# Where q leaves PSUM, where the weight parts are made, and where single steps stand, in a hybrid attention layer

## The chip, the cores and the metric

The kernel runs on one core of one Trainium2 chip. The metric is the device time of one execution in microseconds (us), lower is better. A NeuronCore has five engines with instruction streams of their own: TensorE (PE; its weight loads are listed as PEld), VectorE (DVE), ScalarE (ACT), GpSimd (POOL) and SyncE (SP). Here SyncE and GpSimd issue most of the DMA transfers. Each engine takes its instructions in the order in which the program has them, and waits on semaphores for the others.

## The reference

One layer of a decoder trunk, for 1024 tokens of width 2048, in float32. Cut to what is computed:

```python
hn = rmsnorm(h, norm_mix_g)
sb_q, sb_k, sb_v, sb_g, df_q, df_k, df_v, df_g = split(hn @ w_in)          # eight times 1024 columns
# 8 stick-breaking heads of 128: z = q k / sqrt(128), masked to s < t;
#   w = sigmoid(z_ts) * prod over s<j<t of (1 - sigmoid(z_tj));  out = w @ v
# 8 differential heads, two q/k pairs of 64 each, rotary on the first 16 of each:
#   a = softmax(q1 k1 / 8) - lam * softmax(q2 k2 / 8), causal;  out = a @ v, then rmsnorm over the head
mixed = concatenate([sb_out * silu(sb_g), df_out * silu(df_g)])
h = h + mixed @ w_out
gate = sigmoid(rmsnorm(h, norm_ple_g) @ w_ple_gate)
h = h + gate * (p @ w_ple_proj)
return rmsnorm(h, norm_final_g)
```

## The kernel before, in words

Every large product is done on pairs of numbers. An operand x is cast to a reduced format by ScalarE (the high part, names ending in h or hi), VectorE subtracts that from x (the low part, l or lo), and TensorE adds three products: high by high, high by low, low by high. So each operand costs a 128x512 cast, a 128x512 subtraction and two tiles.

The kernel has four stages.

1. **The seven-product stage for v and g** (class `Seven`, object `gv`, up to about 620 us). It computes the v and gate columns for both halves of the tokens with seven block products instead of eight (A11, A12, S1 to S4, A22), in two phases over the inner dimension and over 16 output units. One product is one *slot* of 12 matmuls. At the end of each slot `step` makes the high and low part of one more weight block (`whigh`, `wlow`), runs what is due, and takes up to two entries of a list of loads and splits. A ring of ten tiles holds the weight parts.
2. **The heads of the first half of the tokens** (`half == 1` in the code; its k and v are kept for the second), about 620 to 1085 us, and then **of the second half** (`half == 0`), to about 1660 us. Heads go in the order `ORDER`: differential head 8, stick-breaking head 0, 9, 1, ..., 15, 7. `unit` computes a head's q and k columns into two PSUM banks (`acc[0]` for q, `acc[1]` for k; the tag has two buffers, so the next head's q product needs the bank that this head's q leaves) in 32 groups of three matmuls. After each group `side.tick()` advances a counter and calls those steps of a sorted list whose tick has come. All other work (casts, scores, softmax, transposes, loads) hangs on that list: `side.add` puts steps at given ticks, `side.later(dt, fn)` puts one dt ticks on. So the attention of a head is done within the product groups of the next two to three heads, and what is called earlier stands earlier in each engine's stream. Equal ticks keep the order in which they were added.
3. **The output projection**, a second `Seven` (`op`). Its first 64 groups (A11 and A12 of eight output units) still carry the last head's attention; their results `hc` go to DRAM.
4. The gate product and the end.

What the change touches, with the lines of the profile:

- `wprep` and `split` load a head's weights (`wraw`, 512 KB), cast them (L162, ScalarE) and, in the first half of the tokens, subtract for the low part (L158, VectorE, 128x1024) and store it in `wlo_d`. The second half loads that stored low part (L164).
- `taken(c)` of a stick-breaking head is called at tick 28 for q and 31 for k. q is cast straight out of PSUM (L1385) and the low part is subtracted from PSUM (L1381). k is first multiplied by the row scale into SBUF (L1377).
- `taken(c)` of a differential head copies q and k to SBUF (L1399), and does the rotary steps and the splits at the ticks `ROPE`. For k these are two 64x512 subtractions into `kl` (L1416) and, behind each, two 64x128 subtractions (L1418) that fill the 128 columns at the end of k, which only a block's last row of scores uses.
- `norm` of a differential head (L519 to L530) makes a mean on TensorE, two ScalarE steps (L523, L524) and four VectorE steps; `mixed` then negates the result on ScalarE (L272) in the first half of the tokens, and stores it.
- At the last head of the first half, `load_x0` loads the other half's x, and splits it (L1152 on ScalarE, L1153 on VectorE).
- `weights_first` loads the weights of the first eight output units (A11 and A12), and casts and subtracts them (L1284, L1287).
- `hc` (L1469) is the copy of an output product out of PSUM, into a ring of four buffers (`f`) that the heads' v, gate and k use too.

TensorE's, VectorE's and ScalarE's instructions stand in the order written out; SyncE's and GpSimd's are placed by the scheduler.

## Time and profile before

| | us |
|---|---|
| median of 3 runs | 2402.86 (2401.71 to 2406.63) |
| the profiled execution | 2402.06 |
| its span, first to last instruction | 2400.2 |
| TensorE busy in it | 2331.9 |
| VectorE busy | 1805.8 |
| ScalarE busy | 1241.2 |
| GpSimd busy | 296.1 |

A busy share is a mean over the stages. TensorE's matmuls of one stream overlap, so that a 128x512 one is listed with about 390 ns. A row of the waits gives who waited for whom, the total in us, how often, and the longest; a row of the order of time gives the start, the duration, the engine, the line, the operation with its tiles, and in brackets the idle time of the engine before it and what ended it. Rows of stretches give each engine's busy time with the number of its instructions, the clock that TensorE was granted (1.00 is full speed), the mean busy share of the DMA engines and GB/s.

### The profile page before, as it was taken

The page shows a single profiled execution, that of the slowest core. Times are in us where ns is not written, and L with a number is a line of the kernel's source. Part 1 is how long each engine was busy: PE and PEld are TensorE (multiplying, and loading weights), DVE is VectorE, ACT ScalarE, POOL GpSimd, SP SyncE. Part 2 cuts the span into 40 slices and gives each one's busy share as a digit, 9 for nine tenths or more (in the row PEclk, how much of TensorE's full clock was granted, in tenths as well). Part 3 has the DMA queues.
Part 4 walks back from the last instruction along what each step waited for, and adds up shares of the span by engine and source line. Part 5 has one row for each costly group of instructions (what it writes and reads, how often), then busy time and mean ns, then how long its engine had stood idle before and what let it go on. Part 6 is the DMA issues. An engine that isn't in the chain of part 4 may idle for free. (4 is left out here: it accounts for less than half of the span.)

```text
span 2400.2 us, 32458 instructions
## 1 busy us (share of the span) xinstructions
PE 2331.9 (97%) x11110; PEld 1939.2 (81%) x11110; DVE 1805.8 (75%) x3171; ACT 1241.2 (52%) x2209; POOL 296.1 (12%) x439
## 2 busy tenths in 40 slices
PE   9999999999999999989999999998899999999998
PEld 7878888888788888777888888887678887888877
DVE  6487676556678888887777877778687988687787
ACT  6322243332466666667666666666542435532455
POOL 1121111111100000000011100111021112011000
PEclk9999999999999999999999999999899999999999
DMA  8585476666887777787667666767598888998965
GB/s 267 205 281 180 147 220 156 145 149 136 226 266 232 244 234 242 245 289 233 191 196 206 175 190 206 198 188 221 123 251 192 255 250 267 311 348 273 329 209 181
DMA packets 241973, 531.47 MB, mean 221 GB/s; under 512 B 27264, under 2 KB 38784, under 8 KB 241808
## 3 DMA queue, kind: packets, MB, share of 16 engines
q1 hardware_dynamic: 172544, 371.01, 47.8%
q0 software_dynamic: 52848, 128.74, 22.0%
q10 hardware_dynamic: 16416, 29.65, 3.4%
q8 instruction: 87, 1.43, 0.2%
q14 instruction: 78, 0.64, 0.1%
HBM read 342.39 MB, written 195.30 MB: 224 GB/s over the span
## 5 line engine op out<-in xcount | busy, mean ns | idle before, releaser
L725 ACT CAST wpr<-T 128x512 fp32r<-128x512 f32 x208 | 126.9, 620 | 485.8 <-DVE T L684 407.1
L240 PE MATMUL acc<-xh,whi 128*128 128x512 f32 x768 | 314.4, 409 | 1.8 <-DVE q L1381 1.7
L242 PE MATMUL acc<-xh,wlo 128*128 128x512 f32 x768 | 301.8, 393 | 1.4 <-DMA wlo<-wlo_d 0.9
L241 PE MATMUL acc<-xl,whi 128*128 128x512 f32 x768 | 301.1, 392 | 0.0
L242 PEld LDWEIGHTS acc<-xh,wlo 128*128 128x128 f32 x768 | 144.6, 188 | 34.6 <-DMA wlo<-wlo_d 1.3
L240 PEld LDWEIGHTS acc<-xh,whi 128*128 128x128 f32 x768 | 145.5, 190 | 27.0 <-ACT xh L1152 1.7
L241 PEld LDWEIGHTS acc<-xl,whi 128*128 128x128 f32 x768 | 145.4, 189 | 23.9 <-issue 0.2
L162 ACT CAST whi<-wraw 128x1024 fp32r<-128x1024 f32 x128 | 134.3, 1049 | 36.5 <-PE acc L241 19.8
L739 DVE TENSOR_TENSOR wpr<-T,wpr 128x512 fp32r<-128x512 f32 x208 | 142.8, 687 | 9.7 <-ACT wpr L725 6.0
L836 POOL DMA_DIRECT2D vg_d<-hc x128 | 89.1, 696 | 453.8 <-DVE hc L1026 261.4
L380 ACT ACTIVATE et<-z,mx 128x512 f32<-128x512 f32 (+7 forms) x128 | 95.0, 742 | 86.9 <-DVE mx L372 86.8
L725 ACT CAST wpr<-wraw 128x512 fp32r<-128x512 f32 x128 | 78.9, 617 | 117.8 <-DMA wraw<-tw_d 38.8
L446 ACT CAST awh<-tp 128x256 fp32r<-128x256 f32 (+1 forms) x160 | 80.5, 503 | 78.9 <-PE tp L427 78.8
L451 DVE TENSOR_TENSOR awl<-tp,awh 128x256 fp32r<-128x256 f32 (+1 forms) x160 | 92.5, 578 | 24.4 <-ACT awh L446 24.4
L739 DVE TENSOR_TENSOR wpr<-wraw,wpr 128x512 fp32r<-128x512 f32 x128 | 87.0, 687 | 30.4 <-ACT wpr L725 30.2
L372 DVE CUSTOM_DVE_ANT_0 z<-z,wide 128x512 f32<-128x512 f32 (+7 forms) x128 | 97.4, 761 | 7.1 <-PE z L324 6.0
L354 DVE TENSOR_TENSOR_SCAN pt<-pt 128x511 f32<-128x511 f32 (+3 forms) x64 | 86.7, 1354 | 15.8 <-ACT pt L347 15.3
L158 DVE TENSOR_TENSOR wlo<-wraw,whi 128x1024 fp32r<-128x1024 f32 x64 | 78.2, 1222 | 13.7 <-ACT whi L162 13.7
L347 ACT ACTIVATE pt<-z,rcol 128x511 f32<-128x511 f32 (+3 forms) x64 | 47.5, 742 | 73.9 <-DVE z L334 73.7
L474 PE MATMUL av<-awl,v 128*128 128x256 f32 x256 | 73.7, 288 | 4.1 <-DVE awl L451 4.1
L472 PE MATMUL av<-awh,v 128*128 128x256 f32 x256 | 72.4, 283 | 0.2
L473 PE MATMUL av<-awh,v 128*128 128x256 f32 x256 | 72.4, 283 | 0.0
(570 smaller groups left out, 6903.9 us busy)
## 6 DMA issues: line engine op xcount, KB each, us to landing
wraw<-w_in SPq DMA_DIRECT2D x128, 512.0 KB, 4.6
wraw<-w_vg SPq DMA_DIRECT2D x143, 256.0 KB, 3.5
vg_d<-hc POOLq DMA_DIRECT2D x128, 256.0 KB, 4.9
wlo_d<-wlo SPq DMA_DIRECT2D x64, 512.0 KB, 3.1
wlo<-wlo_d SPq DMA_DIRECT2D x64, 512.0 KB, 4.2
wraw<-w_gate SPq DMA_DIRECT2D x92, 256.0 KB, 5.4
wraw<-w_out SPq DMA_DIRECT2D x72, 256.0 KB, 4.5
h_d<-hc POOLq DMA_DIRECT2D x56, 256.0 KB, 5.1
```

What stands on the lines that cost most here:

```text
L162: side.later(1, lambda: A.copy(hi[:, o], raw[:, o]))
L240: T.matmul(acc[c], hi[:, k2, kh, c, :], xh, start=first, stop=False)
L241: T.matmul(acc[c], hi[:, k2, kh, c, :], xl, start=False, stop=False)
L242: T.matmul(acc[c], lo[:, k2, kh, c, :], xh, start=False, stop=last)
L354: V.tensor_tensor_scan(pt[:, w], pt[:, w], pt[:, w], initial=1.0, op0=ALU.mult, op1=ALU.bypass)
L372: V.tensor_tensor_reduce(z[:, vw], z[:, vw], add, -DF_SCALE, 3.0e38, ALU.add, ALU.min, mx)
L380: A.activation(et[:, vw], z[:, vw], AF.Exp, bias=mx[:, 0:1], scale=-1.0, accum_out=l[:, c:c + 1])
L446: A.copy(wh[:, o, :], tp[:, o, :])
L451: V.tensor_tensor(wl[:, o, :], tp[:, o, :], wh[:, o, :].bitcast(F32), op=ALU.subtract)
L725: A.copy(t[:, 0], src)
L739: V.tensor_tensor(t[:, 1], src, t[:, 0].bitcast(F32), op=ALU.subtract)
L836: G.dma_start(vg_d[hf, blk, u], o, **(dict(accum_op=ALU.add) if ph else {}))
```

## The change

It has five parts.

1. **q of a stick-breaking head.** ScalarE copies `acc[0]` to SBUF when `taken(0)` is called. The cast and the subtraction read that copy, each one step later than before (1 and 2 ticks after, instead of 0.6 and 1).
2. **The end columns of a differential head's k.** The four 64x128 subtractions on VectorE become four 64x128 ScalarE copies out of `kl` in a step of their own (`ends`, tick 23.5). The two low steps of k move from ticks 21.5 and 23 to 21 and 22.
3. **Chores in the seven-product stage.** From slot 36 on, one block of 128x512 every three slots is loaded, cast, subtracted, and stored: first the 16 blocks of A11 and A12 of `w_out` (both parts, into the new `wout_d`), then the 16 blocks of the q/k weights of the last pair of heads, 15 and 7 (low part only, into `wlo_d`). 32 loads, casts and subtractions, and 48 stores, all DMAs on SyncE.
4. **Their users.** In the first half of the tokens heads 15 and 7 load the low part instead of making it. `weights_first` loads both parts in two DMAs of 512 KB, at the ticks `wf`, into tiles of three rings, and makes nothing.
5. **The ring of `hc`.** Nine of the first output products' copies go to the ring `xt`, the others stay in `f`.

The numbers of all steps move into a table `TICK`; those not named here keep their value.

```diff
+EARLY = ORDER[-2:]
-ROPE = (1.5, 5, 7, 8.5, 12, 14, 15.5), (1.5, 13, 14.5, 16, 19.5, 21.5, 23)
+CHORE = 36
+TICK = {
...
+    "q_turn": (1.5, 5, 7, 8.5, 12, 14, 15.5), "k_turn": (1.5, 13, 14.5, 16, 19.5, 21, 22, 23.5),
...
@@ wprep, split
-            if half == 0:
+            if half == 0 or hd in EARLY:
                 nc.sync.dma_start(lo.bitcast(F32), keep.bitcast(F32))
@@ Seven.step
                 self.due()
+                if self.chore:
+                    self.chore(self.slot)
@@
+        chores = deque()
+        for u in range(8):
+            chores.extend((ap["w_out"][u, 0, k][:, 0], wout_d[u, k, 0], wout_d[u, k, 1]) for k in range(2))
+        for hd in EARLY:
+            for pc in range(4):
+                chores.extend((ap["w_in"][hd][pc][:, o].rearrange("p a b c -> p (a b c)"), None, wlo_d[hd, pc][:, o].rearrange("p a b c -> p (a b c)")) for o in range(2))
+        work = []
+
+        def chore(slot):
+            if slot < CHORE or slot % 3 == 2 and not work:
+                return
+            if slot % 3 == 0 and chores:
+                src, hi_d, lo_d = chores.popleft()
+                raw = ev.tile([P, HALF], F32, name="craw", tag="xt", bufs=4)
+                nc.sync.dma_start(raw, src)
+                work.append([raw, hi_d, lo_d])
+            elif slot % 3 == 1 and work:
+                raw = work[0][0]
+                hi, lo = [ev.tile([P, HALF], F32R, name=nm, tag="xt", bufs=4) for nm in ("chi", "clo")]
+                A.copy(hi, raw)
+                V.tensor_tensor(lo, raw, hi.bitcast(F32), op=ALU.subtract)
+                work[0][0] = hi, lo
+            elif slot % 3 == 2:
+                (hi, lo), hi_d, lo_d = work.pop()
+                if hi_d is not None:
+                    nc.sync.dma_start(hi_d.bitcast(F32), hi.bitcast(F32))
+                nc.sync.dma_start(lo_d.bitcast(F32), lo.bitcast(F32))
@@ weights_first
-                raw = wp.tile([P, 2, 4 * P], F32, name="wraw", tag="wraw", bufs=2)
-                for k in range(2):
-                    nc.sync.dma_start(raw[:, k], ap["w_out"][u, 0, k][:, 0])
-                ...
-                    A.copy(hi[:, k], raw[:, k])
-                    ...
-                        V.tensor_tensor(lo[:, k], raw[:, k], hi[:, k].bitcast(F32), op=ALU.subtract)
+                hl = [pool.tile([P, 2, 4 * P], F32R, name=f"wf{nm}", tag=t, bufs=2) for nm, t in zip(("hi", "lo"), tags)]
+                for i in range(2):
+                    nc.sync.dma_start(hl[i].bitcast(F32), wout_d[u, :, i].bitcast(F32).rearrange("k p n -> p k n"))
+                for k, nm in enumerate(("A11", "A12")):
+                    op.wq[u, 0, nm] = hl[0][:, k], hl[1][:, k]
@@ taken, stick-breaking
-                            f = acc[0]
+                            f = f32t("qk")
+                            A.copy(f, acc[c])
...
-                        side.later(1 if c else 0.6, lambda: A.copy(t[:, 0, :HALF], f))
-                        side.later(2 if c else 1, low)
+                        side.later(TICK["sb_split"][0], lambda: A.copy(t[:, 0, :HALF], f))
+                        side.later(TICK["sb_split"][1], low)
@@ taken, differential
-                            for rr in (r, ro):
-                                V.tensor_tensor(t[rr, b, HALF:], f[r, 3 * P:], t[r, b, 3 * P:HALF].bitcast(F32), op=ALU.subtract)
+                        def ends():
+                            for b, (r, ro) in enumerate(rows):
+                                for rr in (r, ro):
+                                    A.copy(t[rr, b, HALF:], other[r, 0, 3 * P:].bitcast(F32))
...
-                                 high, partial(low, 0), partial(low, 1)]
+                                 high, partial(low, 0), partial(low, 1)] + [ends] * c
@@ first output products
-                    o = ftile()
+                    n = 2 * u + i + 2 * (nm == "A12")
+                    o = ev.tile([P, HALF], F32, name="hc", tag="xt", bufs=4) if n < 9 else ftile()
```

## The prediction

> **What bounds the kernel now.** I read the page's busy shares first, then TensorE's waits (all, and stretch by stretch), then the stretches' busy times, and last the order of time around each wait.

> ```profile
> span 2400.2 us, 32458 instructions
> PE 2331.9 (97%) x11110; PEld 1939.2 (81%) x11110; DVE 1805.8 (75%) x3171; ACT 1241.2 (52%) x2209; POOL 296.1 (12%) x439
> ```

> TensorE is busy for 97% of the span, and the change leaves its instructions and their order as they are. So time comes only out of its waits and the clock behind them.

> ```profile
> PE acc L240 <- DVE q L1381: 13.4, 8, 2.0
> PE av L469 <- DVE lead L450: 10.5, 10, 2.6
> PE z L324 <- DVE kl L1416: 7.2, 2, 6.1
> PE tp L427 <- DVE et L392: 4.3, 8, 1.7
> PE pa L634 <- DVE wflo L1287: 2.4, 1, 2.4
> PE pa L632 <- ACT wfhi L1284: 2.3, 1, 2.3
> PE pa L632 <- ACT hc L1469: 0.7, 1, 0.7
> ```

> Each row is a waiting line, what it waited for, the total, the times and the longest. The edits name the 1st, 3rd, 5th, 6th and 7th directly. By place (columns: stretch, TensorE, its weight loads, VectorE, ScalarE, GpSimd, clock, DMA share, GB/s):

> ```profile
> 180.00:445.00 265.00, 265.00 (x1171) 219.43 (x1170) 177.33 (x278) 85.72 (x148) 38.60 (x57) 1.00 0.63 173
> 605.00:1021.00 416.00, 403.25 (x1963) 336.91 (x1962) 333.33 (x681) 251.29 (x485) 33.37 (x51) 0.99 0.76 243
> 1021.00:1147.00 126.00, 116.08 (x567) 96.75 (x566) 99.94 (x212) 85.69 (x165) 7.81 (x12) 0.97 0.80 258
> 1147.00:1640.00 493.00, 486.11 (x2602) 411.36 (x2601) 382.85 (x685) 330.21 (x543) 50.33 (x70) 1.00 0.67 196
> 1640.00:1770.00 130.00, 107.85 (x527) 86.61 (x526) 96.67 (x167) 78.63 (x144) 16.56 (x21) 0.95 0.65 173
> ```

> TensorE idles 12.8 us in the first half's heads, 9.9 where the halves meet, 6.9 in the second half and 22.1 over the last pair and the first output units. The stage in which the weight parts are now made (180 to 445) has none.

> The clock goes with the waits:

> ```profile
> 726.07:729.48 3.41, 1.46 (x9) 1.00 0.94 347
> 729.48:732.89 3.41, 3.41 (x10) 0.50 0.68 202
> 784.10:787.50 3.40, 1.66 (x9) 1.00 0.96 345
> 787.50:790.90 3.40, 3.17 (x14) 1.00 0.91 322
> ```

> A stretch of 3.41 us with 1.95 idle is followed by one at half clock; one with 1.74 idle is not. A halved stretch of steady work loses 1.7 us. [...]

> **A. q out of PSUM, k's ends on ScalarE (605 to 1021).**

> ```profile
> 726.55 0.63 ACT L272 ACTIVATE neg<-sg 128x512 f32<-128x512 f32 x1 [2.62 <-DVE sg L530]
> 727.09 0.57 ACT L1385 CAST q<-acc 128x512 fp32r<-128x512 f32 x1
> 727.69 0.69 DVE L1381 TENSOR_TENSOR q<-acc,q 128x512 fp32r<-128x512 f32 x1 [0.50 <-ACT q L1385]
> 728.43 0.50 PE L240 MATMUL acc<-cA11h,whi 128*128 128x512 f32 x1 [1.95 <-DVE q L1381]
> 797.13 0.62 DVE L392 SCALAR_TENSOR_TENSOR et<-et,l 128x384 f32<-128x384 f32 x1 [0.54 <-ACT et L387]
> 799.02 0.49 PE L427 MATMUL tp<-ident,et 128*128 128x128 f32 x3
> L485 ACT COPY sm<-av x32: 245/261/267, 720.7 to 1766.4; 128x128 f32<-128x128 f32 x32
> ```

> The next head's product wants q's bank; its last reader is a subtraction behind a cast, behind a negation, behind the norm's last VectorE step. The new copy stands before the negation, where ScalarE idles 2.62 us, so it ends before 726.5, when TensorE wants the bank: the 1.95 us go, six times. Behind the copy q's cast and subtraction come about 0.1 later, with k's read of the second bank after them; that bank is wanted 3 us later, so it is free by some 0.4 us.

> What is late next is the transposition of et. L392 ends at 797.75, TensorE arrives at 799.02: 1.27 of slack, and TensorE now comes 1.95 earlier. Ahead of it, each differential head puts four 64x128 copies on ScalarE before the norm's roots, at most 4 x 0.26 = 1.05 us (L485, nearest in size), at least nothing where ScalarE would idle. I take 0.3 for VectorE's chain, since VectorE is itself still busy for part of them. So 1.95 + 0.3 - 1.27 = 0.98 stays in each pair, and 0.97 x 6 = 5.8 is won, with two halvings (2 x 1.7 = 3.4): **9.2**. Ends: 2 (copies at 1.05, halvings kept) and 15.1 (no wait follows). VectorE's 64 removed subtractions win nothing by themselves, since it waits for ScalarE there.

> **B. Where the halves meet (1021 to 1147).**

> ```profile
> 1070.06 2.56 ACT L1152 ACTIVATE xh<-xl,gvec 128x512 fp32r<-128x512 f32 x4
> 1070.82 1.41 DVE L1153 SCALAR_TENSOR_TENSOR xl<-xl,gvec,xh 128x512 fp32r<-128x512 f32 x2 [2.98 <-ACT xh L1152]
> 1074.96 0.69 DVE L1416 TENSOR_TENSOR kl<-qk,k 64x512 fp32r<-64x512 f32 x1
> 1075.71 0.79 PE L324 MATMUL z<-kl,qz 128*128 128x512 f32 x1 [6.10 <-DVE kl L1416]
> L158 DVE TENSOR_TENSOR wlo<-wraw,whi 128x1024 fp32r<-128x1024 f32 x64 | 78.2, 1222 | 13.7 <-ACT whi L162 13.7
> ```

> Eight L158 of the last pair (8 x 1.22 = 9.8 us of VectorE) become loads, and k's low parts move from 21.5 and 23 to 21 and 22, ahead of the x splits that VectorE sat 2.98 us for. By order alone kl is done some 5 us earlier, and with three L158 gone from the stretch before it, before TensorE asks. The loads replace stores of the same size on SyncE. Gone: 6.1, and 1.5 of the 1.7 that the q wait has outside A (13.4 - 6 x 1.95), and clock of 0.03 x 126 = 3.8: 11.4. But 16 x splits still stand in VectorE's queue; with TensorE some 7 us earlier, k's bank and the first et come late in the turn, 1.5 to 2 each by counting VectorE's rows after kl. Taken: 11.4 - 3.4 = **8**. Ends 5 and 11.4.

> **C. Last pair and first output units (1640 to 1770).**

> ```profile
> L1284 ACT CAST wfhi<-wraw x16: 602/623/671, 1650.3 to 1737.9; 128x512 fp32r<-128x512 f32 x16
> L1287 DVE TENSOR_TENSOR wflo<-wraw,wfhi x16: 668/683/694, 1653.0 to 1740.0; 128x512 fp32r<-128x512 f32 x16
> 1687.75 0.59 ACT L1469 COPY hc<-pa 128x512 f32<-128x512 f32 x1 [4.20 <-DMA h_d<-hc]
> 1640.00:1683.00 43.00, 36.53 (x184) 29.21 (x183) 36.18 (x68) 28.18 (x52) 7.17 (x9) 1.00 0.72 198
> 1683.00:1715.00 32.00, 24.39 (x112) 18.85 (x111) 19.72 (x36) 18.17 (x34) 2.52 (x3) 0.85 0.63 148
> 1715.00:1770.00 55.00, 46.94 (x235) 38.56 (x234) 40.78 (x65) 32.28 (x59) 6.87 (x9) 0.96 0.61 169
> ```

> 16 x 0.62 = 10.0 us of ScalarE and 16 x 0.68 = 10.9 of VectorE leave; 16 loads of double size (both parts) stand in their place, each several output products ahead of its use, so I price them at nothing, at 2 us if a buffer's release holds SyncE. The first nine copies hc leave the ring whose DMA held ScalarE 4.20 us. The three rows give TensorE's idle time as 6.5, 7.6 and 8.1 us. In the middle one 2.3 + 2.4 + 0.7 = 5.4 (the casts, subtractions and hc of the first table) go outright, and about half comes back where the attention's lead waits behind VectorE's scan and the operands' splits: net 2.9. In the first one VectorE, 36.2 of 43 us busy, loses four L1287, their waits for the casts and k's ends: I take 3.9 of 6.5. The last 8.1 hang on splits and scans that stay. Clock: 0.05 x 130 = 6.5, of which half stays, because long waits for lead remain (the longest is 2.6). Sum 2.9 + 3.9 + 3.2 = **10**; ends 4 and 17.

> **D. Second half's heads (1147 to 1640).** No q wait is there to win.

> ```profile
> 1208.08 1.05 ACT L162 CAST whi<-wraw 128x1024 fp32r<-128x1024 f32 x1
> 1211.00 0.69 DVE L527 SCALAR_TENSOR_TENSOR sqv<-msq,avb 128x512 f32<-128x512 f32 x1 [1.02 <-ACT avb L524]
> ```

> The four copies go in before this cast, ScalarE has only a little idle time before the root, and VectorE already waits for that root: some 0.2 later in each of 7 pairs, **-1.4** (ends -4 and 0).

> **E. Making the parts (180 to 445).** 32 times a load, a cast, a subtraction, and 48 stores, of 256 KB: 21 MB in about 260 us, 80 GB/s on 173, a DMA share of about 0.9 for 0.63. VectorE gets 22 us more in 265 where it has 88 free.

> ```profile
> 410.30 0.69 DVE L739 TENSOR_TENSOR wpr<-T,wpr 128x512 fp32r<-128x512 f32 x1
> 412.56 0.39 PE L634 MATMUL pbc<-cS2h,wpr 128*128 128x512 f32 x1
> ```

> The tightest product (S2 in the second phase) has 1.57 us; one subtraction ahead of it leaves 0.88. **0**; ends 0 and -6. On SyncE each store waits for its cast and stands before w_vg loads; the subtraction waits in VectorE's queue for the cast, ahead of the next unit's differences.

> **Sum.** 9.2 + 8 + 10 - 1.4 = 25.8. The profiled execution took 2402.06 (span 2400.2 and 1.9 around it), 0.8 under the median of 2402.86: 2402.1 - 25.8 = 2376.

> **Rivals.**
> 1. The wait only moves: ScalarE, back to back from k's casts to the roots, takes the copies in full. A 2, B 5, C 7, D -4: 10 won, 2392. For it: VectorE's 1.02 wait for the root. Against: the 2.62 idle further on. Chance 0.20.
> 2. No wait follows those removed: 15.1 + 11.4 + 17, 2359. Against: the 1.27 us of slack at et. Chance 0.08.
> 3. The halvings aren't the pauses' doing and stay: 3.4 + 3.8 + 3.2 less, 2386. For it: one pause of 1.74 had none. Against: the clock is 1.00 in the stretch without waits and lowest where they lie densest (0.85 at 1683). Chance 0.07. [...]
> 4. Slower: the chores' DMA delays the stage. When a chore's load, or the w_vg load behind its store, makes S2's parts late beyond 1.57 us, TensorE pauses once in each of eight second-phase units, with 1.7 of clock behind it. From 3.1 us late the gain is gone (8 x 3.2 = 25.8); at 5 us it is 8 x 5.1 = 41, so 2417. For it: share 0.9. Against: TensorE kept full beside shares of 0.94 to 0.96 in the rows at 726 and 784, but for the named wait. Chance 0.11.

> My forecast holds 0.50, from 2364 to 2388; 0.04 is left for no change. Within 0.2% of 2402.9 is about what a measurement can't tell from no change. Faster 0.50 + 0.20 + 0.08 + 0.07 = 0.85; same 0.04; slower 0.11. The range 2357 to 2397 takes in rivals 1 to 3.

> **What would show it.** Right: the row L240 <- DVE q under 1 us; et's wait (L427) grown to about 1 us a pair in the first half; L324 <- kl under 1; no wait on wfhi or wflo; clock 1.00 at 605 to 1021; TensorE 265.00 of 265 still at 180 to 445. Wrong: msq or lead waits of over 1 us a pair (rival 1), or a row of waits on wpr after 180 us (rival 4).

## The result, and the profile after

The changed kernel takes 2396.9 us (median of 7 runs, 2395.46 to 2398.69), the kernel before 2405.24 (7 runs, 2401.71 to 2407.91): a ratio of 0.9968, 95% interval 0.9956 to 0.9979. It is faster by about 8 us. I had forecast 2376, some 26 us faster: under a third of that came. 2396.9 lies just inside the upper end of the range (2357 to 2397), which was drawn wide enough to hold three rivals, so that says nothing for the sum behind 2376.

The page of the profile after, its span and busy times:

```profile
span 2396.9 us, 32668 instructions
PE 2333.0 (97%) x11110; PEld 1934.2 (81%) x11110; DVE 1791.2 (75%) x3115; ACT 1273.9 (53%) x2305; POOL 296.7 (12%) x439
```

VectorE lost 14.6 us of work and ScalarE got 32.7 more. TensorE's time is the same to about 1 us, so the gain is again waits and clock (mean granted clock 0.996 in the profiled execution, 0.993 before). The same stretches as in the prediction (stretch, TensorE, its weight loads, VectorE, ScalarE, GpSimd, clock, DMA share, GB/s), of the kernel after:

```profile
180.00:445.00 265.00, 263.66 (x1160) 217.15 (x1159) 195.09 (x307) 100.79 (x179) 38.66 (x57) 1.00 0.82 246
605.00:1021.00 416.00, 409.25 (x1989) 337.95 (x1989) 326.88 (x655) 263.81 (x523) 34.75 (x52) 1.00 0.76 246
1021.00:1147.00 126.00, 115.49 (x565) 95.39 (x564) 90.92 (x199) 89.83 (x178) 7.84 (x12) 0.99 0.80 254
1147.00:1640.00 493.00, 483.98 (x2584) 407.59 (x2583) 375.34 (x658) 336.90 (x570) 50.42 (x70) 1.00 0.66 195
1640.00:1770.00 130.00, 112.80 (x567) 93.02 (x566) 93.74 (x159) 74.73 (x137) 20.07 (x24) 0.97 0.79 220
```

TensorE's idle time fell from 12.8 to 6.8 us in the first half's heads and from 22.1 to 17.2 in the last stretch. It rose from 9.9 to 10.5 where the halves meet, from 6.9 to 9.0 in the second half, and from 0 to 1.3 in the stage with the chores.

What TensorE waited for in the kernel after, from 605 to 1021, 1021 to 1147, 1147 to 1640, and 1640 to 1770 (total, times, longest):

```profile
PE acc L252 <- DVE qk L1404: 3.2, 6, 0.8
PE acc L254 <- DVE wlo L169: 3.1, 6, 0.5
...
PE acc L254 <- DMA wlo<-wlo_d: 4.6, 3, 2.1
PE acc L252 <- DVE qk L1404: 3.8, 1, 3.8
PE z L336 <- DVE kl L1443: 1.0, 1, 1.0
...
PE tp L438 <- DVE et L403: 3.1, 7, 0.5
...
PE av L480 <- DVE lead L461: 9.0, 3, 4.0
```

The waits for q, wfhi and wflo are gone and kl's fell from 6.1 to 1.0, as meant. New are: k's bank (L1404) and VectorE's weight part (L169) behind the place where q's wait stood; the loads of the low parts and a long wait for k's bank where the halves meet; more than twice the total for et in the second half; and a longer wait for the attention's lead at the end. The last two in the kernel before (1147 to 1640, and 1640 to 1770):

```profile
PE tp L427 <- DVE et L392: 1.4, 6, 0.5
...
PE av L469 <- DVE lead L450: 6.6, 3, 2.6
```

TensorE's 11,110 instructions are the same in the same order in both kernels, so the start of each can be subtracted. The difference between its growth at a stretch's two ends is what that stretch won or lost. By this reckoning, in us, each kernel's profiled execution against that of the kernel before (negative is faster):

| | 180-445 | 605-1021 | 1021-1147 | 1147-1640 | 1640-1770 | 1770-end |
|---|---|---|---|---|---|---|
| my forecast | 0 | -9.2 | -8 | +1.4 | -10 | 0 |
| the changed kernel | +2.4 | -6.6 | +1.0 | +4.2 | -8.8 | +4.2 |
| q's copy alone, on before | 0 | -11.6 | -0.3 | -0.1 | -2.0 | +4.8 |
| k's ends on ScalarE alone, on before | 0 | +5.7 | +1.9 | +3.6 | -1.0 | +5.8 |
| chores alone, on before | +1.7 | -0.7 | +0.6 | -0.3 | +2.1 | +2.5 |
| after, q out of PSUM as before | +2.3 | +17.7 | +0.4 | +3.6 | -8.9 | +4.4 |
| after, ends on VectorE | +2.3 | -11.4 | -2.7 | -0.3 | -8.6 | +4.7 |
| after, ends behind q's copy | +1.0 | -11.2 | -2.1 | -0.4 | -8.4 | +3.0 |
| after, last pair's low parts in place | +0.8 | -6.9 | +0.4 | +4.1 | -9.0 | +4.6 |
| after, output weights made in place | 0 | -6.9 | -1.6 | +4.2 | +0.6 | +3.7 |
| ends on VectorE, low parts loaded first (9) | +1.0 | -11.7 | -2.9 | -0.4 | -7.3 | +2.0 |
| the same, x splits later (10) | +1.7 | -11.6 | -0.2 | -0.5 | -6.6 | +4.1 |
| as 9, q's subtraction behind k's multiply (11) | +2.1 | -14.1 | -3.7 | -0.4 | -8.8 | +4.5 |
| experiments 3, 9 and 11 in one (12) | +1.7 | -13.7 | -3.8 | -0.5 | -8.9 | +3.6 |

I don't count the last column as the change's work: all twelve experiments are 2 to 6 us slower there than the profiled execution of the kernel before, also those that leave that stage as it was. The kernel after has a wait there, in the last 140 us (first fence, 1770 to the end), and so has the kernel before with q's copy alone (second fence):

```profile
PE pc L1763 <- DVE hc L1914: 3.8, 1, 3.8
```

```profile
PE pc L1733 <- DVE hc L1884: 2.9, 1, 2.9
```

The profiled execution of before had no such wait (why is not known), and at 2402.06 it lies 3.2 under its median. So the two profiles differ by 3.4 us (2402.06 to 2398.69) where the medians differ by 8.3; the sum of the other columns, -7.8, agrees with the medians.

### The profile page after: what moved, and what is told of

It reads as the page before. It is cut to its first block, busy times and chain, and to the rows that moved or that the text cites. A ratio compares the mean times of both kernels' runs of the same rounds, so it can differ in the third digit from the quotient of the medians.

```text
span 2396.9 us, 32668 instructions
## 1 busy us (share of the span) xinstructions
PE 2333.0 (97%) x11110; PEld 1934.2 (81%) x11110; DVE 1791.2 (75%) x3115; ACT 1273.9 (53%) x2305; POOL 296.7 (12%) x439
## 4 chain that ended last, share of the span: by engine, by line
PE 65%; DVE 15%; issue 8%; ACT 7%; DMA 3%; POOL 1%; SPq 0%; ACTq 0%; DVEq 0%; POOLq 0%
PE acc L252 5%; PE acc L254 5%; PE acc L253 5%; PE pbc L650 4%; PE pbc L648 4%; PE pbc L649 4%; PE pc L650 2%; PE pc L649 2%; PE pa L648 2%; PE pc L648 2%; PE pa L650 2%; PE pa L649 2%; DVE z L383 2%; PE pb L1765 2%; PE pb L1764 2%
## 5 line engine op out<-in xcount | busy, mean ns | idle before, releaser
L254 PE MATMUL acc<-xh,wlo 128*128 128x512 f32 x768 | 301.6, 393 | 5.1 <-DMA wlo<-wlo_d 4.6
L254 PEld LDWEIGHTS acc<-xh,wlo 128*128 128x128 f32 x768 | 144.5, 188 | 39.4 <-DMA wlo<-wlo_d 6.3
L173 ACT CAST whi<-wraw 128x1024 fp32r<-128x1024 f32 x128 | 134.4, 1050 | 35.7 <-PE acc L253 20.0
L366 DVE TENSOR_TENSOR_SCAN pt<-pt 128x511 f32<-128x511 f32 (+3 forms) x64 | 86.6, 1354 | 17.2 <-ACT pt L359 16.7
L169 DVE TENSOR_TENSOR wlo<-wraw,whi 128x1024 fp32r<-128x1024 f32 x56 | 68.5, 1223 | 16.8 <-ACT whi L173 16.1
L485 PE MATMUL av<-awl,v 128*128 128x256 f32 x256 | 74.1, 289 | 3.5 <-DVE awl L462 3.5
```

The lines of the kernel that those rows point to most:

```text
L173: side.later(1, lambda: A.copy(hi[:, o], raw[:, o]))
L254: T.matmul(acc[c], lo[:, k2, kh, c, :], xh, start=False, stop=last)
```

## The experiments

Each was timed against the kernel before on the same chip; the kernel before had medians of 2404.4, 2405.3 and 2404.9 us in the three sets.

**1. k's ends back on VectorE.** The four 64x128 copies are subtractions again, at the changed kernel's places.

```diff
+                            for rr in (r, ro):
+                                V.tensor_tensor(t[rr, b, HALF:], f[r, 3 * P:], t[r, b, 3 * P:HALF].bitcast(F32), op=ALU.subtract)
...
-                                 high, partial(low, 0), partial(low, 1)] + [ends] * c
+                                 high, partial(low, 0), partial(low, 1)]
```

> The changed kernel, but k's 64x128 ends are subtractions on VectorE again (L1416 of the kernel before), at the new places. Theory 1, the four copies on ScalarE cost the second half's heads: TensorE's wait for et falls from 0.49 to 0.2 us a pair, and 1147 to 1640 takes about 4 us less than in the changed kernel; 605 to 1021 is within 1 us of it. About 2393. Theory 2, the loss in the second half comes from q's copy: et's wait stays at 0.5 a pair, and the time at 2397.

Measured: 2388.24, ratio 0.9929 (0.9914 to 0.9943), 8.7 under the changed kernel. Theory 1 holds in the second half (4.5 us). For the first half's heads, which it had within 1 us of the changed kernel, it was wrong: there the copies cost 4.8, and where the halves meet 3.7. The wait for k's bank there is gone and the one for et is back to 0.2 a pair. This kernel, 605 to 1018 and 1147 to 1640:

```profile
PE acc L254 <- DVE wlo L169: 2.6, 6, 0.5
...
PE tp L438 <- DVE et L403: 1.2, 6, 0.2
```

**2. The same edit alone, on the kernel before.** The ends become ScalarE copies at 24.5, nothing else.

> The kernel before with one edit: k's ends are four copies on ScalarE, at 24.5 behind the low parts at 21.5 and 23. Theory 1, the copies stand on ScalarE ahead of the norm's roots and delay the chain to q by 0.9 us a pair: the wait for q grows from 1.95 to about 2.85, each pause is now followed by a halved clock, and 605 to 1021 takes about 19 us more, 1147 to 1640 about 4 more: about 2425. Theory 2, they cost the 0.3 a pair that I forecast: 2407.

Measured: 2425.39, ratio 1.0077 (1.0061 to 1.0094), 20 us slower than before. The size of theory 1 came out, and its 2.85 us a pause (this kernel, 605 to 1018):

```profile
PE acc L240 <- DVE q L1381: 14.4, 5, 3.0
```

The part on the clock did not: in the profiled execution the granted clock at 605 to 1021 was 0.99, where six halved stretches of 3.41 us would leave 0.975 (an estimate: 6 x 3.41 x 0.5 us lost of 416), and that stretch took 5.7 more and not 19. One pause was followed by half clock (0.50 from 730.30 to 733.70), another was not (1.00 from 791.74 to 795.16). But the profiled execution took 2418.2, 7 under the median. The four longest (2425.1 to 2429.1) had a mean granted clock of 0.986 to 0.989, where the profiled one had 0.992. As an estimate, that part of some 2425 us is 7 to 15 us more lost to the clock. So theory 1's halvings may have come in those; where they fell was not profiled.

**3. The ends at another place.** The four copies stay on ScalarE, but are issued directly behind the copy of the next short head's q.

```diff
-                                 high, partial(low, 0), partial(low, 1)] + [ends] * c
+                                 high, partial(low, 0), partial(low, 1)] + [lambda: late.append(ends)] * c
...
                             A.copy(f, acc[c])
+                            while late:
+                                late.pop()()
```

> The changed kernel, but the four copies of k's ends (4 x 0.30 = 1.2 us) are issued directly behind q's copy of the next short head, where ScalarE idles 1.8 to 2.6 us for the norm's last step, and no longer ahead of the norm's roots. Theory 1, their place costs: 605 to 1021 takes 5 us less than in the changed kernel, 1147 to 1640 4 us less, as with the ends on VectorE, and about 2388 in all. Theory 2, ScalarE's added work costs wherever it stands (q's cast and the attention's exponentials come later): less than half of it comes back, 2393 or more.

Measured: 2384.8, ratio 0.9922 (0.9908 to 0.9936), 12 under the changed kernel. Theory 1. The same work at another place costs nothing that shows. ScalarE around one pair, in order of time, first the kernel after, then this one:

```profile
778.70 0.62 ACT L1436 CAST k<-qk 64x512 fp32r<-64x512 f32 x1
779.33 1.28 ACT L224 ACT_TABLE_LOAD   x1
780.63 0.27 ACT L496 COPY sm<-av 128x128 f32<-128x128 f32 x1
780.92 1.23 ACT L1450 CAST k<-kl 64x128 fp32r<-64x128 f32 x4
782.17 1.06 ACT L173 CAST whi<-wraw 128x1024 fp32r<-128x1024 f32 x1
783.13 0.68 ACT L534 ACTIVATE avb<-msq,eps 128x512 f32<-128x512 f32 x1
...
785.05 0.58 ACT L1400 COPY qk<-acc 128x512 f32<-128x512 f32 x1
787.42 0.63 ACT L284 ACTIVATE neg<-sg 128x512 f32<-128x512 f32 x1 [1.79 <-DVE sg L541]
```

```profile
780.17 0.68 ACT L534 ACTIVATE avb<-msq,eps 128x512 f32<-128x512 f32 x1
782.54 1.23 ACT L1454 CAST k<-kl 64x128 fp32r<-64x128 f32 x4
784.79 0.63 ACT L284 ACTIVATE neg<-sg 128x512 f32<-128x512 f32 x1 [1.02 <-DVE sg L541]
```

In the kernel after there is no bracket, so no idle time, from k's casts to the copy of q: each microsecond put in there moves the norm's root (L534), and with it the norm, `neg`, q's cast and all that stands behind them. With the ends on VectorE (experiment 1) the same root starts 1.21 us earlier than in the kernel after, though TensorE starts the same product at 774.6 and 774.7 in the two:

```profile
781.92 0.68 ACT L534 ACTIVATE avb<-msq,eps 128x512 f32<-128x512 f32 x1
```

Behind q's copy the 1.23 us lie in ScalarE's idle time, which shrinks from 1.79 to 1.02.

**4. q's copy alone, on the kernel before.**

```diff
-                            f = acc[0]
+                            f = f32t("qk")
+                            A.copy(f, acc[c])
```

> The kernel before with one edit: q of the short heads leaves PSUM by the ScalarE copy (cast and subtraction at 1 and 2 after it). Theory 1, this copy alone is the whole gain of the first half's heads and k's ends only took from it: 605 to 1021 takes 11 to 13 us less than before, the granted clock there is 1.00; where the halves meet the wait for kl (6.1) stays or grows, since TensorE comes earlier; 1147 to 1640 as before. About 2392. Theory 2, q's copy too makes what follows late: 605 to 1021 wins 6.6 as in the changed kernel, and 1147 to 1640 loses: 2398 or more.

Measured: 2394.52, ratio 0.9959 (0.9946 to 0.9971): theory 1, also the 6.2 us for kl, which stay. This one edit gains some 11 us, no less than the whole change did (the two intervals overlap). What is late next is VectorE's low part of the weights, 0.5 us at most (this kernel, 605 to 1018):

```profile
PE acc L242 <- DVE wlo L158: 3.0, 7, 0.5
```

**5. The changed kernel without q's copy**, at q's old places.

```diff
-                            f = f32t("qk")
-                            A.copy(f, acc[c])
+                            f = acc[0]
...
-                        side.later(TICK["sb_split"][0], lambda: A.copy(t[:, 0, :HALF], f))
-                        side.later(TICK["sb_split"][1], low)
+                        side.later(TICK["sb_split"][0] if c else 0.6, lambda: A.copy(t[:, 0, :HALF], f))
+                        side.later(TICK["sb_split"][1] if c else 1, low)
```

> The changed kernel, but q is read from PSUM by its split again, at the old places (cast 0.6 and subtraction 1 after its take). Theory: six waits of 1.95 for q at 605 to 1021 return, the waits for k's bank (0.5 to 0.8 each) and for wlo (0.5 each) go with them, and the granted clock falls to 0.99 again: that stretch takes 6 to 7 us more, and at 1085 the 3.84 for k's bank goes but 1.5 for q comes. About 2402. Rival: the second half's heads (et, +0.7 a pair) are slower through q's copy; then 4 us come back there and the time is 2398.

Measured: 2416.23 (2405.73 to 2426.1), ratio 1.0047 (1.003 to 1.0065). I missed by 14: the pauses for q come back with 2.85 us and not 1.95, since the ends still delay the root, and in the profiled execution (2422.4, 6 above the median) the granted clock at 605 to 1021 is 0.96. One pause is followed by 6.8 us at half clock (0.50 from 793.30 to 800.10); five like it, the number of these waits from 605 to 1018, would leave 0.959, as an estimate (5 x 6.8 x 0.5 us lost of 416). Without q's copy the rest of the change is a loss. The rival gets no support: 1147 to 1640 is as slow as in the changed kernel.

**6. The last pair's low parts made in place.**

```diff
-EARLY = ORDER[-2:]
+EARLY = []
```

> The changed kernel, but the last pair's low parts are made in its own stretch again (eight subtractions L169 of 1.22 us return to VectorE at 1021 to 1147, their eight loads go, and the eight chores for them). Theory 1, the gain where the halves meet was eaten by these loads landing late: the waits of L254 for the load of wlo (1.28 and 2.10 us in the trace after) go, k's ends stay on time because their places were moved, and the stretch 1021 to 1147 takes some 4 us less than in the changed kernel: about 2393. Theory 2, the early parts are what got kl done in time: TensorE waits for kl 3 us or more again, and the stretch takes 0 to 4 us more: about 2397 to 2401. The pause of 1.05 us at 333 should go in neither.

Measured: 2396.08, ratio 0.9963 (0.9948 to 0.9977): not to be told from the changed kernel. Each theory named a half. The waits for the loads go, the wait for kl rises from 1.0 to 3.5, and the longest wait for k's bank falls from 3.8 to 1.3; the stretch takes 0.6 less. So the early parts for the last pair gain nothing here: what VectorE saves is lost at the loads and at k's bank. The pause at 333 fell to 0.2, which neither theory had.

**7. The output units' weights made in place.** `weights_first` and its places are those of the kernel before, and the chores for the last pair alone are left.

```diff
-        for u in range(8):
-            chores.extend((ap["w_out"][u, 0, k][:, 0], wout_d[u, k, 0], wout_d[u, k, 1]) for k in range(2))
...
+                    A.copy(hi[:, k], raw[:, k])
...
+                        V.tensor_tensor(lo[:, k], raw[:, k], hi[:, k].bitcast(F32), op=ALU.subtract)
...
-                    o = ev.tile([P, HALF], F32, name="hc", tag="xt", bufs=4) if n < 9 else ftile()
+                    o = ftile()
```

> The changed kernel, but the first output units' weights are cast and subtracted in 1640 to 1770 again, with the copies hc in their old ring; of the chores the eight for the last pair stay. My reading of the trace after: the waits for wfhi and wflo (2.3 and 2.4) return, 1640 to 1770 loses the 8.8 us that it won, and the chores' pause of 1.3 us at 333 goes or stays. About 2404. Rival: the new wait of 4.0 for the attention's lead shows that VectorE and ScalarE bound this stretch anyway; then less than 4 us are lost: under 2401.

Measured: 2401.65, ratio 0.9984 (0.9975 to 0.9993). 1640 to 1770 loses 9.4 us against the changed kernel, so the price of the parts was right, though the time lies between my reading (2404) and the rival's (under 2401). The pause in the chores' stage goes (2.4 us), and 1021 to 1147 is 2.6 us shorter, which I can't explain by the edit.

**8. The chores alone, on the kernel before.** `chore` and its list are added as in the change; the stored parts are read by nobody, those of the last pair go to a spare array.

```diff
+                if self.chore:
+                    self.chore(self.slot)
...
+                chores.extend((ap["w_in"][hd][pc][:, o].rearrange("p a b c -> p (a b c)"), None, spare_d[hd, pc][:, o].rearrange("p a b c -> p (a b c)")) for o in range(2))
```

> The kernel before, with the changed kernel's chores in the seven-product stage (32 loads, casts, subtractions and 48 stores), whose results nobody reads. Theory 1, as in the trace after: one pause of 1 to 1.3 us near 331 with its clock, 180 to 445 takes 1 to 3 us more, all else is unchanged: 2405 becomes 2407. Theory 2, my rival 4: eight pauses in the second phase, 2415 or more. Theory 3, nothing: within 1 us.

Measured: 2407.59, ratio 1.001 (1.0001 to 1.0019), about 2.6 us slower: theory 1, for the time and for the pause. The profile also has 2.1 more at 1640 to 1770, where no chore stands; that is not explained. In the chores' stage TensorE waits once (1.0), for VectorE's read of a product's bank. In the kernel after (first ScalarE and VectorE at the chore before it, then the wait's own place, in order of time):

```profile
327.23 0.62 ACT L1055 CAST chi<-craw 128x512 fp32r<-128x512 f32 x1 [2.62 <-DMA craw<-w_out]
...
327.89 0.69 DVE L1056 TENSOR_TENSOR clo<-craw,chi 128x512 fp32r<-128x512 f32 x1 [2.85 <-ACT chi L1055]
...
334.03 0.69 DVE L1056 TENSOR_TENSOR clo<-craw,chi 128x512 fp32r<-128x512 f32 x1
...
334.63 0.69 DVE L1111 TENSOR_TENSOR u<-pbc,s 128x512 f32<-128x512 f32 x1
```

A chore's load is late, its cast holds ScalarE for 2.62, its subtraction holds VectorE for 2.85, and VectorE, back to back from there, comes to the next bank (L1111) behind one more chore's subtraction.

**9. The low parts loaded first.** On experiment 1, the new x blocks of the halves' meeting are asked for one place later, with their splits where they were.

```diff
-                    side.add([(8 * pc + 7, partial(swap, pc)) for pc in range(4)])
+                    side.add([(8 * pc + 8, partial(swap, pc)) for pc in range(4)])
-    "x0": (5, 6, 13, 14),
+    "x0": (4, 5, 12, 13),
```

> The changed kernel with k's ends on VectorE, and the new x blocks of the halves' meeting loaded one place later, so that the load of the next low parts stands ahead of them on SyncE (their splits keep their places). Theory 1, the low parts were late because four 256 KB loads stood before them: the 2.3 us of waits of L254 for the load of wlo go, and 1021 to 1147 takes 2 to 3 us less than in the kernel with ends on VectorE alone: 2386. Theory 2, the load is late because the 16 engines are full (share 0.99 at 1050 to 1070) and its buffer comes free one chunk ahead, whatever the order: no change, 2388.

Measured: 2385.04, ratio 0.9916 (0.9903 to 0.9929), 3 under experiment 1, which their intervals don't tell apart. And the profile doesn't place the 3 us there: the waits for these loads fall from 2.3 to 1.0, kl's rises from 0.4 to 2.0, and 1021 to 1147 takes only 0.2 less than in experiment 1. Neither theory is shown. The DMA engines' share of 0.99 that theory 2 names for 1050 to 1070 is 0.91 in the profile of the kernel after. On SyncE the load moved ahead of one x block only, since the scheduler places that queue.

**10. The x splits four places later too**, on experiment 9.

```diff
-    "x0": (4, 5, 12, 13),
+    "x0": (8, 9, 16, 17),
```

> As the kernel with the low parts loaded first, and the x splits four places later, behind k's read of its bank. Theory 1, the 3.8 us wait for k's bank near 1080 is VectorE's queue (four splits of 0.7 that wait for ScalarE's): it falls under 1.5, the stretch wins 2 to 3 us more, 2383. Theory 2, the splits are then late for the next unit's products, or their ScalarE part delays the roots: a new wait of 1 us or more on xl or et in 1060 to 1110, and 2386 or more.

Measured: 2391.22, ratio 0.994 (0.9928 to 0.9952): theory 2 in time. k's bank still costs 2.7, and the attention's lead and et now cost 2.5 and 1.6. So k's bank does not wait for the splits alone.

**11. q's subtraction behind k's multiply**, on experiment 9.

```diff
-                        side.later(TICK["sb_split"][1], low)
+                        side.later(TICK["sb_split"][1] if c else 4.5, low)
```

> The kernel with ends on VectorE and the low parts loaded first (2385), with q's subtraction issued behind k's multiply instead of ahead of it. Theory 1, k's bank is late because VectorE's read of it stands behind q's subtraction, which waits 0.5 for q's cast: the 3.8 us wait near 1080 falls by 0.7 to 1.2 and the 0.5 waits for wlo in 605 to 1021 shrink: 2383 to 2384. Theory 2, k's bank waits for the x splits, and the attention's lead now comes behind q's subtraction: no gain, 2385 to 2388.

Measured: 2381.65, ratio 0.9905 (0.9892 to 0.9919). Theory 1 for the first half's heads, which win 2.4 more (-14.1 in all); the total for wlo there falls from 2.6 to 0.5. Near 1075 k's bank still waits 3.2, where experiment 9 had 3.8: theory 1 was too high there.

**12. Experiments 3, 9 and 11 in one kernel.**

> The changed kernel with the ends behind q's copy, the low parts loaded first, and q's subtraction behind k's multiply. Theory 1, the three are separate: about 2383. Theory 2, with the copies on ScalarE behind q's copy, q's cast is late for the subtraction and for the scores: 2388 or more.

Measured: 2384.01 (2380.24 to 2385.18), ratio 0.9912 (0.9899 to 0.9926). Theory 1. With the order of experiments 9 and 11, the ends behind q's copy are no better than on VectorE: 11 and 12 can't be told apart by their times. Either is some 13 to 15 us faster than the changed kernel. Here k's bank waits 1.1 where experiment 11 had 3.2, but kl and et then wait 2.0 and 1.8 (1.3 and 0.9 there), and 1021 to 1147 is as long (this kernel, 1018 to 1147):

```profile
PE z L336 <- DVE kl L1447: 2.0, 1, 2.0
PE tp L438 <- DVE et L403: 1.8, 1, 1.8
PE acc L252 <- DVE qk L1408: 1.1, 1, 1.1
```

## Why the prediction was wrong

It had the direction, and the gains of A and C. By the table the five stretches won 7.8 us where I had 25.8. Of the 18.0 that are missing, 12.9 are the price of putting the four copies of k's ends on ScalarE there: with the ends on VectorE (experiment 1) the same stretches win 20.7. By the medians of those two kernels, timed in different sets, the copies cost 8.7. Most of the rest is missing in B, which won 2.7 in that kernel where I had 8.

- **A, q and k's ends (forecast 9.2, measured 6.6).** q's half was right: the copy stands before the negation, the six waits go, and so does the clock's loss (1.00 at 605 to 1021, where the kernel before had 0.99). Alone it won 11.6. The step that failed is "I take 0.3 for VectorE's chain, since VectorE is itself still busy for part of them". The copies took 1.23 us (4 x 0.30; I had taken 4 x 0.26 from L485), and cost 0.8 us a pair (4.8 over six). I had placed them "before the norm's roots", and had looked for ScalarE's idle time only behind them; the rows under experiment 3 show that there is none ahead. I also named the wrong wait that follows. TensorE does not reach the transposition of et with its 1.95 us: it waits before that for k's bank (0.5 to 0.8, with the ends) and for VectorE's subtraction of the weights (0.5). "Free by some 0.4 us" for k's bank was wrong with the ends on ScalarE; without them no wait for it is left (experiment 1). Without the copies 3.7 of the 15.1 still stay, mostly at that subtraction of the weights, and I had 4.1 for it at et (0.68 x 6): near in size by luck. The low end of 2 was also too high by its own numbers, which give 1.3 (0.22 x 6).
- **D, the second half (forecast -1.4, measured -4.2, just past my end of -4).** The same term: 0.2 a pair was taken, 0.6 was measured, and with the ends elsewhere the loss is gone (experiments 1 and 3).
- **B, where the halves meet (forecast 8, measured -1.0, outside my ends of 5 and 11.4).** The waits that go, go: in TensorE's start times kl gives 5.1 us, the half clock behind it (0.50 from 1074.23 to 1081.06 in the kernel before) 2.4 (I had 3.8) and q 1.8. The step that failed is "the loads replace stores of the same size on SyncE", priced at nothing, and "1.5 to 2 each" for what comes late. The loads took 4.3 back, k's bank 5.0 (0.9 and 4.1), and a half clock behind it (0.50 from 1084.65 to 1088.06 in the kernel after) 1.4. TensorE waits for these loads, as it did not for the stores, and the buffer of each is released only one weight block ahead: from 1021 to 1100 SyncE's queue waited for TensorE's last use of one six times, 14.3 us in all. Here they stand behind the new x blocks on SyncE and share the DMA engines with them (busy share 0.89 from 1050 to 1062). The kernel after, SyncE's queue ahead of the longest wait, and that wait:

```profile
1051.15 1.00 SPq L1196 DMA_DIRECT2D xl<-h_d  x2
1052.21 0.42 SPq L1366 DMA_DIRECT2D vf<-vg_d  x1
1052.68 0.90 SPq L1196 DMA_DIRECT2D xl<-h_d  x2
1053.67 0.38 SPq L175 DMA_DIRECT2D wlo<-wlo_d  x1
...
1062.13 0.50 PE L254 MATMUL acc<-xh,wlo 128*128 128x512 f32 x1 [2.10 <-DMA wlo<-wlo_d]
```

  From issue to landing such a load took 7.1 us here (median, 1023 to 1071; 3.3 to 8.9); in the second half of the kernel before, 4.2. Which of the two makes a load late, its place or the share, is not shown (experiment 9). With the ends moved, B still wins only 2 to 4 us, so the term would have been wrong without them. What holds k's bank for 3 us is VectorE, in the kernel after:

```profile
1080.53 1.41 DVE L1200 SCALAR_TENSOR_TENSOR xl<-xl,gvec,xh 128x512 fp32r<-128x512 f32 x2 [1.32 <-ACT xh L1199]
1081.86 0.69 DVE L383 CUSTOM_DVE_ANT_0 z<-z,wide 128x512 f32<-128x512 f32 x1
1082.47 0.14 DVE L383 DVE_READ_ACCUMULATOR2_ANT mx<- 128x1 f32 x1
1082.47 1.41 DVE L1200 SCALAR_TENSOR_TENSOR xl<-xl,gvec,xh 128x512 fp32r<-128x512 f32 x2
1083.79 0.69 DVE L1408 TENSOR_TENSOR q<-qk,q 128x512 fp32r<-128x512 f32 x1
1084.39 0.69 DVE L1404 TENSOR_TENSOR qk<-acc,ssa 128x512 f32<-128x512 f32 x1
```

  Its read (L1404) stands behind splits that wait for ScalarE, which waits for the norm. Moving q's subtraction and the splits shortened that wait by some 1 us each at most (experiments 10 and 11). In experiment 12 it fell to 1.1, and kl and et waited longer instead. What sets the length of this stretch stays open.
- **C, the last stretch (forecast 10, measured 8.8).** Near in its sum, and experiment 7 gave 9.4 back. The parts were not right: the first 43 us gave 1.8 where I had 3.9, the next 32 gave 8.0 where I had 2.9 and the clock's share, and the last 55 lost 0.9. That they add up is partly luck. As forecast, part of it returned at the attention's lead, whose total rose from 6.6 to 9.0.
- **E, the chores (forecast 0, measured -2.4, within my ends).** The mechanism is that of rival 4, once and not eight times: 1.05 us of wait, and the rest around it.
- **The rivals.** Rival 1, the copies taken in full, came nearest (2392, with 7 for C and -4 for D), and it had 0.20. At A its 2 was further from the 6.6 than my 9.2, and its sign did not come: in the second half's heads msq waits 0.3 at most and lead 0.6, as before. Its ground, VectorE's wait of 1.02 for the root, was the row to go by. My counter, the 2.62 us of idle time "further on", answered for work put there, and the copies were put ahead of it.
- **The signs.** No wait for q, wfhi or wflo, and the clock of 1.00 at 605 to 1021, came as named; kl came to 1.0. Et's 1 us a pair in the first half and TensorE's 265.00 in the chores' stage did not.

## What to carry to other kernels

Before work is moved to an engine that is idle on average, read that engine's queue between the last wait and the instruction that somebody waits for. Here the four small copies cost 9 to 12 us at one place and nothing measurable 3 us later, in the same engine's idle time. That a store of the same size went did not make the load free here (4.3 us came back): ask how long before its use its buffer is released, and what stands ahead of it in its queue. And time each part of a change alone: here q's copy alone gained 10.8 us and all five edits together 8.3, with intervals that overlap.

## What the runs showed of the hardware

```profile
789.88:793.30 3.42, 1.28 (x8) 0.84 (x6) 2.81 (x7) 1.17 (x3) 0.00 (x0) 1.00 0.89 316
793.30:796.70 3.40, 2.69 (x7) 2.30 (x8) 2.09 (x7) 2.40 (x7) 0.00 (x0) 0.50 0.98 328
796.70:800.10 3.40, 3.40 (x10) 2.63 (x9) 3.40 (x7) 1.49 (x3) 0.68 (x1) 0.50 0.58 201
```

```profile
784.91:788.33 3.42, 2.16 (x12) 1.56 (x10) 3.10 (x5) 1.15 (x4) 0.00 (x0) 1.00 0.84 303
788.33:791.74 3.41, 1.83 (x8) 1.59 (x9) 1.86 (x6) 2.41 (x7) 0.00 (x0) 1.00 0.86 307
791.74:795.16 3.42, 3.42 (x18) 2.87 (x17) 3.16 (x7) 2.37 (x5) 0.68 (x1) 1.00 0.51 168
```

The clock records and TensorE's idle time (by the profile's matmul ends) of the profiled executions of the kernel before and the kernel after, cut along this grid up to the last halving, agree with that. Of the stretches at full clock, all 9 with more than 2.0 us idle were followed by half clock, 2 of the 7 with 1.55 to 2.0, and none of the 1369 with less. A stretch at half clock was followed by another where it held 0.92 us or more of idle time (0.7 in the rows without q's copy), and by full clock where it held 0.49 or less. So the pause of 2.85 with 2.1 us in one stretch and 0.7 in the next cost two halved stretches, and the two of 1.95 that ended inside their stretch cost one each.

The executions of the changed kernel without q's copy spread from 2405.7 to 2426.1. That spread goes with the clock: its mean was 0.994 in the shortest of the twelve and 0.986 in the longest, an estimated 19 us of some 2410, and the times differ by 20. That the place of the pauses in the grid is behind it was not shown, since one execution was profiled.
